# Two hybrid decoder layers on one core: linear attention's buffers laid on those of the attention's projections, its gates split by token half, and an earlier, wider spaced stream of cache pages

## The chip, the cores and the metric

The kernel runs on one core of one Trainium2 chip. The metric is the device time of one execution in microseconds; lower is better. Runs of the kernel before agree within 0.1%.

## What is computed

Two consecutive layers of a decoder, for a prompt of 1024 tokens and for 8 single sample tokens that share the weights, all in float32 (each large product is made of three matmuls on split high and low halves). The core of the reference, for the prompt:

```python
n = rmsnorm(yp, norm1[l])
q, k, v, gq, gk, gv, glog, gg = project(n, w_in[l], ...)      # one input projection, two groups of heads
od = diff_attn_prompt(q, k, v, lam)        # softmax(q1 k1^T) - lam * softmax(q2 k2^T), times v; 4 heads
og, s_fin = gla_prompt(gq, gk, gv, glog)   # S_t = diag(alpha_t) S_{t-1} + k_t^T v_t;  o_t = q_t S_t; 4 heads
yp = yp + merge(od, og, gg, ...)           # og -> rmsnorm(og) * silu(gg); concat(od, og) @ w_out
yp = yp + ffn(yp, norm2[l], w_gu[l], w_down[l])               # (silu(a) * b) @ w_down, width 2816
```

The 8 sample tokens go through the same layer; their attention reads 1024 past keys and values each from a paged cache (8 pages of 128 rows x 512 per token, for keys and for values), and their linear attention updates a given state by one step.

## The kernel before

Tiles are handed out by pools with a compile-time scheduler: instructions are issued on each engine in the order in which a simulated run finds them ready, the lowest priority number first. A pool with `reuse_waits="tile"` lets a new tile wait only for the old tiles that lay on the same bytes or banks. Pools are stacked from the left of the on-chip memory, and from the right with `side="right"`, so the order in which they are opened decides what lies on what.

Each layer (`layer`, L265) has three stages.

- **Attention** (`phase_d`, L383): for each of 4 heads, 9 projection tiles (`psq`, weights in `wDr`, `wDh`, `wDl`: raw, high half, low half), and two tiles later scores (`psS`), softmax, transposes (`tpw`) and the product with v (`po`). Its banks are `psS` 0 to 2, `psT` 3 and 4, `psg` 5 to 7.
- **Linear attention** (`phase_g`, L605): products for q and k (`psqk`), v (`psv`) and the gate (`psgg`), all from pool `psgg`, with weights in `wGr`, `wGh`, `wGl`; log gates, six levels of decay masks (`gla_a`), the chunk recurrence (`gla_o`), a norm per token half (`gate_norm`, `psgn`), and the product with silu of the gate. For the second pair of heads the gate of all tokens is kept in `gqs[0]`, and `gate_mul(t)` applies it to the token half t. The order of these calls is written out at the end of the function. `PIECES` cuts the tokens into 512, 260 and 260 (the 8 sample tokens are the last).
- **Out-projection and feed-forward**, for tokens 0 to 511 and then for the other 520 (`out_half`, `ffn_half`). Here priorities are planned times: `dense(us)` (L100) gives each weight tile its place on a clock of TensorE time (2.8 us for half an out-projection tile, 5.6 for a tile of the gate or up product, 0.7 per row block of the down product), and `mix(us)` (L104) the place of the sample tokens' work on the same clock. `prep_tile` loads a weight tile over SP into `raw` (3 buffers), casts its high half on ACT into `wh` and its low half on DVE into `wl`, and notes the three instructions in `marks`; `behind(slot)` queues an instruction behind the one noted for the current place, on the same engine.

`decode` (L1090) runs beside the first half's feed-forward, from `MIX_START` on the planner's clock: 64 key pages (load over SP, product with `qbd` on GpSimd, reduction `sall` on DVE), the softmax over all, 64 value pages (even ones on ACT and GpSimd, odd ones on DVE, summed in `vacc`), and twice `sample_gla`, the state step of two heads (loads of the states `S0` and of `vb`, four products and sums on GpSimd, a store). Its pool `dec` lies at the right, below the accumulators of the out-projection. The 8 tokens' result `osf` goes into the second half's `out_half`, whose pool `op` lies on the bytes of `dec`.

Of the kernel before, what the change touches and what calls it, by code (L numbers as in the profile page):

```python
# [10 lines left out]
F32 = mybir.dt.float32  # L11
# [7 lines left out]
PSUM = bass.MemoryType.PSUM  # L19
DRAM = bass.MemoryType.DRAM  # L20

P = 128
# [9 lines left out]
WM = HALF + NB  # L32
PIECES = ((0, HALF), (HALF, HALF + WM // 2), (HALF + WM // 2, TOK))
TICK = 20
MIX_START = 58.0
DEPTH = 2
PAST = 1024
NPG = 8
# [2 lines left out]
DK = 64  # L41
DV = 128
RANK = 16
NPB = 6
LAG = 2
GRH = 3
VPOOL = (0, 2, 4, 6)
# [15 lines left out]
def hybrid_kernel(  # L63
# [201 lines left out]
    def layer(l):  # L265
        sn = smp.tile([NB, 2 * H], F32, name="sn", tag="sn")
        osf = smp.tile([P, 2 * H, NB], F32, name="osf", tag="osf")
        smc = smp.tile([P, 2, 3, NB], F32, name="smc", tag="smc")
        gsm = smp.tile([P, H, NB], F32, name="gsm", tag="gsm")
        if l:  # L270
            sample_cols()

        with ExitStack() as octx:
            with ExitStack() as mix_:
                pgp = mix_.enter_context(tc.tile_pool(name="pgp", bufs=1, reuse_waits="tile", side="right"))
                with ExitStack() as dctx:
                    wa2 = phase_d(l, dctx, sn, pgp)
                ogb = octx.enter_context(tc.tile_pool(name="ogb", bufs=1, reuse_waits="tile"))
                og1 = ogb.tile([P, H, WM], F32, name="og1", tag="og1")
                oga = octx.enter_context(ExitStack())  # L280
                ogp = oga.enter_context(tc.tile_pool(name="oga", bufs=1, reuse_waits="tile"))
                og0 = ogp.tile([P, H, HALF], F32, name="og0", tag="og0")
                ogs = (og0, og1)
                with ExitStack() as gctx:
                    phase_g(l, gctx, ogs, smc, gsm, wa2)
            with ExitStack() as pctx:
                psD = pctx.enter_context(tc.tile_pool(name="psD", bufs=2, space=PSUM, reuse_waits="tile"))
                psn = pctx.enter_context(tc.tile_pool(name="psn", bufs=2, space=PSUM, reuse_waits="tile"))
                psX = pctx.enter_context(tc.tile_pool(name="psX", bufs=2, space=PSUM, reuse_waits="tile"))
                wps = [pctx.enter_context(tc.tile_pool(name=n, bufs=1, reuse_waits="tile", side="right")) for n in ("wFr", "wFh", "wFl")]  # L290
                span_start()
                with ExitStack() as fctx:
                    with ExitStack() as actx:
                        ac = new_acc(actx)
                        acc = out_half(l, 0, og0, osf, ac, wps, psD)
                        oga.close()
                        ffn_half(l, 0, acc, ac, wps, psD, psn, fctx)
                        clock["mix"] = MIX_START
                        decode(l, actx, osf, smc, gsm, psX)
                    actx = pctx.enter_context(ExitStack())  # L300
                    ac = new_acc(actx)
                    acc = out_half(l, 1, og1, osf, ac, wps, psD)
                ffn_half(l, 1, acc, ac, wps, psD, psn, actx)
                span_end()
# [298 lines left out]
        return wa2  # L603

    def phase_g(l, gctx, ogs, smc, gsm, wa2):  # L605
        psg = gctx.enter_context(tc.tile_pool(name="psgg", bufs=2, space=PSUM, reuse_waits="tile"))
        gp, gpd, gl, ge_, wr, wh_, wl_, gqp, gb_ = [gctx.enter_context(tc.tile_pool(name=n, bufs=1, reuse_waits="tile"))
                                          for n in ("gp", "gpD", "gpL", "gpE", "wGr", "wGh", "wGl", "gqp", "gpB")]
        wp = (wr, wh_, wl_)
        psA = gctx.enter_context(tc.tile_pool(name="psA", bufs=2, space=PSUM, reuse_waits="tile"))  # L610
        psO = gctx.enter_context(tc.tile_pool(name="psOg", bufs=1, space=PSUM, reuse_waits="tile"))
        psX = gctx.enter_context(tc.tile_pool(name="psXg", bufs=1, space=PSUM, reuse_waits="tile"))
        psT = gctx.enter_context(tc.tile_pool(name="psTg", bufs=2, space=PSUM, reuse_waits="tile"))

        gr = ssq[0:RANK, :]
        gqs = [(pl.tile([P, TOK], F32, name=f"gq{p}", tag=f"gq{p}"), pl.tile([P, TOK], F32, name=f"gk{p}", tag=f"gk{p}"))
# [211 lines left out]

        gws = {}

        def gate_proj(p, e):
            store = p == 1
            if p not in gws:
                gws[p] = prep_cols(wp, l, C_GG + p * 256, 1, 256, 256, q=w_queues[2])
            Hs, Ls = gws[p]
            for t, (ca, cb) in enumerate(PIECES):
                n = cb - ca
                ps = psg.tile([P, 512], F32, name="psgg", tag="g")
                gemm_feat(ps, e * P, Hs, Ls, t)
                y = gqs[0][e][:, ca:cb] if store else gpd.tile([P, HALF], F32, name="gy", tag="gy", bufs=1)[:, :n]  # L840
                tt(y, ps[:, :n], rstd[:, ca:cb], ALU.mult)
                a = gb_.tile([P, 512], F32, name="gya", tag="gsq", bufs=2)[:, :n]
                act(a, y, AF.Abs)
                act(a, a, AF.Exp, scale=-1.0)
                act(a, a, AF.Ln, bias=1.0)
                stt(a, y, 0.0, a, ALU.min, ALU.subtract)
                act(a, a, AF.Exp)
                tt(y, y, a, ALU.mult)
                if t == 2:
                    DVE.tensor_copy(gsm[:, 2 * p + e, :], y[:, n - NB:n])  # L850
                if not store:
                    m = n - (NB if t == 2 else 0)
                    o = ogs[0][:, 2 * p + e, :] if t == 0 else ogs[1][:, 2 * p + e, ca - HALF:ca - HALF + m]
                    tt(o, o, y[:, :m], ALU.mult)
# [27 lines left out]
        gla_o(1, 1, 0)  # L882
        gla_o(1, 1, 1)
        gate_norm(1, 0)
        gate_proj(1, 0)
        gate_proj(1, 1)
        gate_mul(0)
        gate_norm(1, 1)
        gate_mul(1)

    def new_acc(st):
# [195 lines left out]

    def decode(l, st, osf, smc, gsm, psX):  # L1090
        cp = st.enter_context(tc.tile_pool(name="dec", bufs=1, reuse_waits="tile", side="right"))
        sall = cp.tile([P, NPG, NB, 2 * H], F32, name="sall", tag="sall")
        wall = cp.tile([P, NPG, 32], F32, name="wall", tag="wall")
        wnb = cp.tile([P, 32], F32, name="wnb", tag="wnb")
# [6 lines left out]

        def decode_k(b):
            qb = cp.tile([P, 512], F32, name="qbd", tag="qb", bufs=2)
            SP.dma_start(qb, scr_q[l][b:b + 1, :].to_broadcast([P, 512]))
            for j in range(NPG):
                mix(2.1)
                pg = page(cache_k[l], b, j)
                tt(pg, pg, qb, ALU.mult, POOL)
                with behind(3, 1):
                    DVE.tensor_reduce(out=sall[:, j, b, :], in_=pg.rearrange("p (h d) -> p h d", d=DK), axis=AX.X, op=ALU.add)  # L1110
# [4 lines left out]
        def sample_gla(p):  # L1115
            q, k, eg = (smc[:, p, a, :] for a in range(3))
            sh = [P, 4, DV]
            vbs = []
            for b0 in (0, 4):
                bs = slice(b0, b0 + 4)  # L1120
                S0 = cp.tile(sh, F32, name="S0", tag="S0", bufs=1)
                vb = cp.tile(sh, F32, name="vb", tag="vb", bufs=2)
                for e in range(2):
                    h = 2 * p + e
                    SP.dma_start(S0[64 * e:64 * e + 64], state_gla[l, bs, h].rearrange("b d v -> d b v"))
                    SP.dma_start(vb[64 * e:64 * e + 64],
                                 scr_gv[l][bs, h * DV:(h + 1) * DV].unsqueeze(0).to_broadcast([64, 4, DV]))
                tt(S0, S0, bc(eg[:, bs].unsqueeze(2), sh), ALU.mult, POOL)
                tt(vb, vb, bc(k[:, bs].unsqueeze(2), sh), ALU.mult, POOL)
                tt(S0, S0, vb, ALU.add, POOL)  # L1130
                for e in range(2):
                    SP.dma_start(gla_sample[l, bs, 2 * p + e].rearrange("b d v -> d b v"), S0[64 * e:64 * e + 64])
                tt(vb, S0, bc(q[:, bs].unsqueeze(2), sh), ALU.mult, POOL)
                vbs.append(vb)

            def out():
                ps = psx("pss")
                pv = ps[:, 0:16].rearrange("p (b e) -> p b e", e=2)
                for b in range(NB):
                    mm(pv[:, b, :], vbs[b // 4][:, b % 4, :], hsel, True, True)  # L1140
                DVE.tensor_copy(osf[:, H + 2 * p:H + 2 * p + 2, :], pv.rearrange("p b e -> p e b"))

            return out
# [41 lines left out]
            tt(osd, pn[:, 32:64].rearrange("p (h b) -> p h b", h=H), wnb.rearrange("p (b h) -> p h b", h=H), ALU.mult)  # L1185

        def decode_v(b):
            acc = cp.tile([P, H, DV], F32, name="vacc", tag="prod", bufs=4)
            accp = cp.tile([P, H, DV], F32, name="vaccp", tag="qb", bufs=2)
            first = {0: True, 1: True}  # L1190
            for j in range(NPG):
                mix(2.1)
                pg = page(cache_v[l], b, j)
                w4 = wall[:, j, b * H:(b + 1) * H]
                p4 = pg.rearrange("p (h d) -> p h d", h=H)
# [42 lines left out]
        for b in range(NB):  # L1238
# [1 line left out]
            if len(ready) > 2:  # L1240
                ready.pop(0)()
            if b in (1, 4):
                mix(6)
                gla = sample_gla(b // 4)
            if b in (3, 6):
                gla()
# [79 lines left out]
```

## Time and profile before

| | us |
|---|---|
| runs (median, lowest, highest of 3) | 2836.69, 2835.61, 2837.54 |
| the profiled execution, its own time | 2846.13 |
| its span, first to last instruction | 2844.3 |
| TensorE matmul busy | 2723.1 (96%) |
| VectorE (DVE) busy | 1804.5 (63%) |
| ScalarE (ACT) busy | 1361.1 (48%) |
| GpSimd (POOL) busy | 386.3 (14%) |
| mean granted TensorE clock | 0.985 |

Layer 0 runs to about 1425 us and layer 1 from there on. In layer 0 the attention ends near 312, the linear attention near 539, the first token half near 996. TensorE is the engine that the others serve; a stretch in which its busy time falls short of the stretch, or in which its granted clock is below 1, is where time is lost. A line of the timeline gives start, duration, engine, source line, operation, output and inputs, the count of equal instructions that follow one another, and in brackets how long the engine had been idle and what ended that.

### The profile page before, as it was taken

How to read it: one execution, taken by the hardware profiler on the slowest of the kernel's cores; microseconds unless marked ns; L12 is line 12 of the kernel's file. 1: busy time of each engine (PE TensorE's matmuls, PEld its weight loads, DVE VectorE, ACT ScalarE, POOL GpSimd, SP SyncE). 2: the span in 40 equal slices, each digit the busy share in tenths (PEclk: the TensorE clock that was granted, in tenths of full speed). 3: DMA queues.
4: the chain of work that ended last, by engine and by line, in shares of the span. 5: the costliest groups of instructions: out<-in, count | busy, mean ns of one | idle time of the engine just before them, and what ended most of it. 6: DMA issues, size and time to landing. Idle time of an engine off the chain costs nothing.

```text
span 2844.3 us, 46804 instructions
## 1 busy us (share of the span) xinstructions
PE 2723.1 (96%) x16906; PEld 2406.7 (85%) x16906; DVE 1804.5 (63%) x3549; ACT 1361.1 (48%) x3343; POOL 386.3 (14%) x333
## 2 busy tenths in 40 slices
PE   7999899998999999999999999999999999999999
PEld 6887788777788799999988878877677888999999
DVE  6777676568877564444478765775678765544444
ACT  7888445532455343222278883464324453322222
POOL 1000000046433000000020000000663320000000
PEclk9999999999999999999999999999999999999999
DMA  4121111266666342333222111112666664333332
GB/s 132 55 62 36 52 32 44 68 176 210 208 190 195 103 133 83 96 91 96 71 53 58 41 36 47 31 47 84 201 208 205 178 189 137 93 91 90 96 90 83
DMA packets 461322, 298.13 MB, mean 105 GB/s; under 512 B 34698, under 2 KB 416906, under 8 KB 461090
## 3 DMA queue, kind: packets, MB, share of 16 engines
q1 hardware_dynamic: 452322, 290.90, 34.6%
q10 hardware_dynamic: 8704, 4.20, 0.5%
q8 instruction: 134, 2.20, 0.3%
q14 instruction: 98, 0.80, 0.1%
q0 software_dynamic: 64, 0.03, 0.0%
HBM read 271.53 MB, written 23.53 MB: 104 GB/s over the span
## 4 chain that ended last, share of the span: by engine, by line
PE 72%; DVE 12%; ACT 8%; issue 3%; DMA 3%; POOL 2%; SPq 0%; DVEq 0%; ACTq 0%; POOLq 0%
PE psd L82 51%; PE psq L82 4%; PE psv L82 3%; PE psqk L82 3%; DVE wl L135 2%; PE psgg L82 2%; PE po L82 2%; ACT sc L88 2%; POOL page L135 1%; ACT qn L88 1%; ACT qhh L88 1%; PE poG L82 1%; PE psS L82 1%; PE tpw L85 1%; DMA page<-in_cache_k 1%
## 5 line engine op out<-in xcount | busy, mean ns | idle before, releaser
L88 ACT ACTIVATE wh<-raw 128x512 fp32r<-128x512 f32 (+1 forms) x608 | 354.1, 615 | 937.8 <-PE psd L82 697.2
L82 PE MATMUL psd<-xH,wl 128*128 128x260 f32 (+1 forms) x2112 | 681.0, 322 | 16.0 <-DVE wl L135 16.0
L82 PE MATMUL psd<-xH,wh 128*128 128x260 f32 (+1 forms) x2112 | 677.9, 321 | 0.0
L82 PE MATMUL psd<-xL,wh 128*128 128x260 f32 (+1 forms) x2112 | 676.8, 321 | 1.0 <-DVE xL L138 1.0
L135 DVE TENSOR_TENSOR wl<-raw,wh 128x512 fp32r<-128x512 f32 (+1 forms) x608 | 454.2, 764 | 90.3 <-issue 51.4
L82 PEld LDWEIGHTS psd<-xH,wl 128*128 128x128 f32 x2112 | 398.5, 189 | 53.2 <-DVE wl L135 22.0
L82 PEld LDWEIGHTS psd<-xL,wh 128*128 128x128 f32 x2112 | 398.1, 188 | 34.2 <-DVE xL L138 2.7
L82 PEld LDWEIGHTS psd<-xH,wh 128*128 128x128 f32 x2112 | 398.0, 189 | 30.2 <-issue 0.5
L82 PE MATMUL psd<-hh,wl 128*128 128x260 f32 (+1 forms) x1056 | 341.6, 323 | 15.4 <-DVE wl L135 15.1
L82 PE MATMUL psd<-hh,wh 128*128 128x260 f32 (+1 forms) x1056 | 340.5, 322 | 1.0 <-DVE acc L135 1.0
L82 PE MATMUL psd<-hl,wh 128*128 128x260 f32 (+1 forms) x1056 | 339.7, 322 | 0.0
L82 PEld LDWEIGHTS psd<-hh,wl 128*128 128x128 f32 x1056 | 200.5, 190 | 35.5 <-DVE wl L135 21.2
L135 DVE TENSOR_TENSOR acc<-psd,acc 128x520 f32<-128x520 f32 (+1 forms) x144 | 125.7, 873 | 163.0 <-PE psd L82 162.8
L82 PEld LDWEIGHTS psd<-hh,wh 128*128 128x128 f32 x1056 | 200.5, 190 | 15.4 <-issue 1.3
L82 PEld LDWEIGHTS psd<-hl,wh 128*128 128x128 f32 x1056 | 200.4, 190 | 14.3
L135 POOL TENSOR_TENSOR page<-page,qbd 128x512 f32<-128x512 f32 x128 | 191.5, 1521 | 59.4 <-DMA page<-in_cache_k 41.9
L82 PE MATMUL psq<-wh,xH 128*128 128x384 f32 (+1 forms) x512 | 178.7, 349 | 6.6 <-DVE zs L135 3.1
L82 PE MATMUL psq<-wh,xL 128*128 128x384 f32 (+1 forms) x512 | 178.3, 349 | 0.0
L82 PE MATMUL psq<-wl,xH 128*128 128x384 f32 (+1 forms) x512 | 177.6, 347 | 0.0
L135 DVE TENSOR_TENSOR sa<-psd,rstd 128x520 f32<-128x520 f32 (+1 forms) x66 | 57.6, 873 | 180.2 <-PE psd L82 176.1
L135 DVE TENSOR_TENSOR tb<-psd,rstd 128x520 f32<-128x520 f32 (+1 forms) x66 | 57.6, 873 | 152.2 <-PE psd L82 152.2
L138 DVE SCALAR_TENSOR_TENSOR wl<-raw,g1c,wh 128x256 fp32r<-128x256 f32 (+2 forms) x160 | 80.7, 537 | 88.4 <-ACT wh L88 52.6
(330 smaller groups left out, 5386.1 us busy)
## 6 DMA issues: line engine op xcount, KB each, us to landing
raw<-in_w_gu SPq DMA_DIRECT2D x176, 512.0 KB
raw<-in_w_down SPq DMA_DIRECT2D x160, 256.0 KB
page<-in_cache_k SPq DMA_DIRECT2D x128, 256.0 KB
page<-in_cache_v SPq DMA_DIRECT2D x128, 256.0 KB
raw<-in_w_out SPq DMA_DIRECT2D x32, 512.0 KB
raw<-in_w_in SPq DMA_DIRECT2D x64, 192.0 KB
raw<-in_w_in SPq DMA_DIRECT2D x64, 128.0 KB
xt<-in_x_prompt SPq DMA_DIRECT2D x8, 512.0 KB
```

What stands on the lines that cost most here:

```text
L82: PE.matmul(out, lhsT=lhsT, rhs=rhs, start=start, stop=stop, skip_group_check=True)
L85: PE.matmul(out, lhsT=in_, rhs=ident[:n, :n], is_transpose=True)
L88: return ACT.activation(out, in_, func, **kw)
L135: return (eng or DVE).tensor_tensor(out, a, b, op=op)
L138: (eng or DVE).scalar_tensor_tensor(out=out, in0=in0, scalar=scalar, in1=in1, op0=op0, op1=op1)
```

## The change

Four things are changed.

1. In `phase_g` the pools of the masks and decay buffers (`gl`, `ge`) are opened after the weights, `gqp` and `gpB` instead of before, so that weights and `gqp` move down by their 14 KB. The psum pool `psgg` is opened last instead of first: its two banks become 6 and 7 instead of 0 and 1, and the four others move down by two.
2. `gate_proj` takes the pieces that it is to make. For the second pair of heads the piece of the first token half is made for both columns, then the norm of the second half, `gate_mul(0)`, and then the other pieces.
3. `decode` gets its pool from the caller, which opens it before the first out-projection; the value accumulators are three tiles of their own instead of four of a ring, and page buffers are 5 instead of 6, so that the pool is 4 KB smaller.
4. The sample work starts at 24 instead of 58 on the planner's clock, with 2.6 us instead of 2.1 for each page. The loads of `qbd`, `S0` and `vb` are queued behind the weight load of their place; the state's place is 5 us for each half of the tokens instead of 6 ahead of both; the state's store is queued behind the weight load due 10 us later.

```diff
-MIX_START = 58.0
+MIX_START = 24.0
-NPB = 6
+NPB = 5
@@ layer
                         ac = new_acc(actx)
+                        cp = actx.enter_context(tc.tile_pool(name="dec", bufs=1, reuse_waits="tile", side="right"))
                         acc = out_half(l, 0, og0, osf, ac, wps, psD)
...
-                        decode(l, actx, osf, smc, gsm, psX)
+                        decode(l, cp, osf, smc, gsm, psX)
@@ phase_g
-        psg = gctx.enter_context(tc.tile_pool(name="psgg", bufs=2, space=PSUM, reuse_waits="tile"))
-        gp, gpd, gl, ge_, wr, wh_, wl_, gqp, gb_ = [gctx.enter_context(tc.tile_pool(name=n, bufs=1, reuse_waits="tile"))
-                                          for n in ("gp", "gpD", "gpL", "gpE", "wGr", "wGh", "wGl", "gqp", "gpB")]
+        gp, gpd, wr, wh_, wl_, gqp, gb_, gl, ge_ = [gctx.enter_context(tc.tile_pool(name=n, bufs=1, reuse_waits="tile"))
+                                          for n in ("gp", "gpD", "wGr", "wGh", "wGl", "gqp", "gpB", "gpL", "gpE")]
...
         psT = gctx.enter_context(tc.tile_pool(name="psTg", bufs=2, space=PSUM, reuse_waits="tile"))
+        psg = gctx.enter_context(tc.tile_pool(name="psgg", bufs=2, space=PSUM, reuse_waits="tile"))
...
-        def gate_proj(p, e):
+        def gate_proj(p, e, ts=(0, 1, 2)):
...
-            for t, (ca, cb) in enumerate(PIECES):
+            for t in ts:
+                ca, cb = PIECES[t]
...
         gate_norm(1, 0)
-        gate_proj(1, 0)
-        gate_proj(1, 1)
+        gate_proj(1, 0, (0,))
+        gate_proj(1, 1, (0,))
+        gate_norm(1, 1)
         gate_mul(0)
-        gate_norm(1, 1)
+        gate_proj(1, 0, (1, 2))
+        gate_proj(1, 1, (1, 2))
         gate_mul(1)
@@ decode
-        cp = st.enter_context(tc.tile_pool(name="dec", bufs=1, reuse_waits="tile", side="right"))
+        vaccs = [cp.tile([P, H, DV], F32, name=f"vacc{z}", tag=f"vacc{z}") for z in range(3)]
@@ decode_k
-            SP.dma_start(qb, scr_q[l][b:b + 1, :].to_broadcast([P, 512]))
+            with behind(1):
+                SP.dma_start(qb, scr_q[l][b:b + 1, :].to_broadcast([P, 512]))
             for j in range(NPG):
-                mix(2.1)
+                mix(2.6)
@@ sample_gla, for each half of the tokens
+                mix(5)
+                with behind(1):
+                    for e in range(2):
+                        h = 2 * p + e
+                        SP.dma_start(S0[64 * e:64 * e + 64], state_gla[l, bs, h].rearrange("b d v -> d b v"))
...
-                for e in range(2):
-                    SP.dma_start(gla_sample[l, bs, 2 * p + e].rearrange("b d v -> d b v"), S0[64 * e:64 * e + 64])
+                with tc.issue_after(mark_at(clock["mix"] + 10)[1].ins):
+                    for e in range(2):
+                        SP.dma_start(gla_sample[l, bs, 2 * p + e].rearrange("b d v -> d b v"), S0[64 * e:64 * e + 64])
@@ decode_v
-            acc = cp.tile([P, H, DV], F32, name="vacc", tag="prod", bufs=4)
+            acc = vaccs[b % 3]
...
-                mix(2.1)
+                mix(2.6)
@@ the loop over value requests
             if b in (1, 4):
-                mix(6)
                 gla = sample_gla(b // 4)
```

## Rows read from the trace of the kernel before

**Rows 1.** The page's engine line: busy us, share of the span, instructions.
```profile
PE 2723.1 (96%) x16906; PEld 2406.7 (85%) x16906; DVE 1804.5 (63%) x3549; ACT 1361.1 (48%) x3343; POOL 386.3 (14%) x333
```

**Rows 2.** Busy by stretch: PE, PEld, DVE, ACT, POOL (count); PEclk, DMA share, GB/s.
```profile
284.00:355.00 71.00, 60.20 (x354) 50.87 (x354) 46.50 (x105) 33.67 (x70) 5.80 (x10) 0.93 0.18 52
```

**Rows 3.** TensorE's waits, 287 to 319: us in total, times, longest.
```profile
PE tpw L85 <- DVE sc L138: 3.7, 2, 3.2
PE psqk L82 <- DVE wl L138: 3.2, 1, 3.2
PE psN L82 <- ACT sqo L88: 1.1, 1, 1.1
```

**Rows 4.** Timeline of TensorE: behind the wait, and 4 us later.
```profile
315.49 0.63 PE L82 MATMUL psqk<-xH,wl 128*128 128x512 f32 x1
315.92 0.63 PE L82 MATMUL psqk<-xH,wh 128*128 128x512 f32 x1
...
319.08 0.39 PE L82 MATMUL psqk<-xL,wh 128*128 128x512 f32 x1
319.31 0.40 PE L82 MATMUL psqk<-xH,wl 128*128 128x512 f32 x1
```

**Rows 5.** TensorE's waits at the same place of layer 1, 1694 to 1726.
```profile
PE psqk L82 <- DVE wl L138: 4.3, 1, 4.3
```

**Rows 6.** Timeline of DVE and of ACT at the end of attention.
```profile
313.13 1.67 DVE L138 SCALAR_TENSOR_TENSOR wl<-raw,g1c,wh 128x256 fp32r<-128x256 f32 x4
...
306.46 0.39 ACT L88 ACTIVATE oraw<-po 128x256 f32<-128x256 f32 x1 [4.62 <-PE po L82]
```

**Rows 7.** Busy by stretch, and timeline of TensorE, into the first out-projection.
```profile
530.00:547.00 17.00, 10.97 (x25) 6.29 (x24) 8.26 (x16) 9.39 (x18) 0.00 (x0) 0.70 0.23 63
1937.00:1954.00 17.00, 11.46 (x27) 6.65 (x26) 8.38 (x16) 9.51 (x19) 0.00 (x0) 0.60 0.22 62
...
532.98 3.61 PE L82 MATMUL psgn<-gsq,ones_dv 128*128 128x512 f32 x4 [2.60 <-ACT gsq L88]
539.06 0.50 PE L82 MATMUL psd<-oHb,wh 128*128 128x512 f32 x1 [2.48 <-ACT wh L88]
```

**Rows 8.** Timeline of SP and of ACT: the out-projection's weights.
```profile
456.68 0.43 SPq L896 DMA_DIRECT2D raw<-in_w_out  x1
...
537.88 3.22 ACT L88 ACTIVATE wh<-raw 128x512 fp32r<-128x512 f32 x6
```

**Rows 9.** TensorE's waits, 568 to 710, then 1975 to 2150 (layer 1).
```profile
PE psd L82 <- DVE wl L135: 13.1, 7, 5.0
...
PE psd L82 <- DVE wl L135: 14.3, 10, 4.6
```

**Rows 10.** Timeline of GpSimd, DVE and TensorE while key pages stream.
```profile
609.61 1.04 POOL L135 TENSOR_TENSOR vb<-vb,smc 128x512 f32<-128x512 f32 x1 [2.70 <-DMA vb<-scr_gv]
...
615.44 0.69 DVE L1110 TENSOR_REDUCE sall<-page 128x8 f32<-128x512 f32 x1 [6.04 <-POOL page L135]
...
676.59 1.04 POOL L135 TENSOR_TENSOR S<-S,smc 128x512 f32<-128x512 f32 x1 [4.96 <-DMA S<-in_state_gla]
...
683.15 0.63 PE L82 MATMUL psd<-hh,wl 128*128 128x512 f32 x1 [4.10 <-DVE wl L135]
```

**Rows 11.** DVE's casts, 545 to 569 (GpSimd idle) and 595 to 760.
```profile
L135 DVE TENSOR_TENSOR wl<-raw,wh 128x512 fp32r<-128x512 f32 x7 | 4.6, 686 | 12.7 <-issue 9.9 <-PE psd L82 2.8
...
L135 DVE TENSOR_TENSOR wl<-raw,wh 128x512 fp32r<-128x512 f32 x51 | 55.4, 1106 | 9.6 <-issue 5.3 <-DMA vb<-scr_gv 2.4 <-ACT wh L88 1.8
```

**Rows 12.** Timelines of SP, ACT, TensorE at decode's end; SP's waits, 585 to 760.
```profile
902.71 0.33 SPq L312 DMA_DIRECT2D page<-in_cache_v  x1
...
936.61 0.21 ACT L88 ACTIVATE oHa<-osf 128x32 fp32r<-128x32 f32 x1
...
998.78 0.59 PE L82 MATMUL psd<-oHb,wh 128*128 128x260 f32 x1 [2.20 <-ACT wh L88]
...
SPq L312 <- DVE sall L1110: 15.7, 13, 3.2
```

More of the change, by code (lines that the diff above doesn't have):

```diff
@@ L1086, in ffn_half, with decode @@
         down(end, he)
-    def decode(l, st, osf, smc, gsm, psX):
-        cp = st.enter_context(tc.tile_pool(name="dec", bufs=1, reuse_waits="tile", side="right"))
+    def decode(l, cp, osf, smc, gsm, psX):
+        vaccs = [cp.tile([P, H, DV], F32, name=f"vacc{z}", tag=f"vacc{z}") for z in range(3)]
         sall = cp.tile([P, NPG, NB, 2 * H], F32, name="sall", tag="sall")
@@ L1122, in sample_gla @@
                 vb = cp.tile(sh, F32, name="vb", tag="vb", bufs=2)
-                for e in range(2):
[L1124 to L1127, printed above, removed]
+                mix(5)
[3 more added lines that the diff above has]
+                        SP.dma_start(S0[64 * e:64 * e + 64], state_gla[l, bs, h].rearrange("b d v -> d b v"))
+                        SP.dma_start(vb[64 * e:64 * e + 64],
+                                     scr_gv[l][bs, h * DV:(h + 1) * DV].unsqueeze(0).to_broadcast([64, 4, DV]))
                 tt(S0, S0, bc(eg[:, bs].unsqueeze(2), sh), ALU.mult, POOL)
@@ L1130, in sample_gla @@
                 tt(S0, S0, vb, ALU.add, POOL)
-                for e in range(2):
-                    SP.dma_start(gla_sample[l, bs, 2 * p + e].rearrange("b d v -> d b v"), S0[64 * e:64 * e + 64])
+                with tc.issue_after(mark_at(clock["mix"] + 10)[1].ins):
+                    for e in range(2):
+                        SP.dma_start(gla_sample[l, bs, 2 * p + e].rearrange("b d v -> d b v"), S0[64 * e:64 * e + 64])
                 tt(vb, S0, bc(q[:, bs].unsqueeze(2), sh), ALU.mult, POOL)
```

## The prediction, made before the change was run

> **What bounds the kernel now.** I read the page's engine line first, then the busy time by stretch, then TensorE's waits in the stretches where it falls short, then the timeline inside those. TensorE is busy 96% of the span, every other engine 63% or less [rows 1]. So what can be won is TensorE's idle time and the slow clock after it. Both stand in three places of each layer: where attention hands over to the linear attention (71 - 60.2 = 10.8 us idle in 284 to 355, granted clock 0.93) [rows 2], where the linear attention hands over to the out-projection, and in the first third of the first half's feed-forward, while key pages stream. The change touches these three and takes no work off TensorE, so the sum is three terms per layer. [...]
>
> **Term 1: attention to linear attention.** TensorE waits 3.7 us for the last score rows, 1.1 for their norm, and 3.2 for `wl`, the low half of the first q/k weights [rows 3]: 8.0 us. Behind the last gap some eight 512-column matmuls lose 0.2 us each, and narrow ones and the last `po` run at half pace; with 3.5 us for this (an estimate from [rows 4]) the place costs 11.5 us in layer 0. Layer 1 waits 4.3 for the same casts [rows 5]; I count 11 there.
> Why does the work behind it not fill this? The first `wl` casts run at 313.13, four in one block [rows 6]. Before, most of `wGl` and all of `gqp` lie on attention's buffers (pool `dpB`) and `psgg` on the score banks (`psS`), in use until the last head is finished. After, the weight pools, `gqp` and the gemm banks lie inside those of attention's own projection (`wDr`, `wDh`, `wDl`, `psg`), whose last matmul comes before attention's last two tiles. So eight casts on ACT and eight on DVE, at some 0.45 us each, can be done in gaps such as ACT's 4.62 us wait for `po` [rows 6], and 22 us of `psqk` matmuls (48 of 512 columns at 0.23 us and 96 of 260 at half that) are there as filler. But `raw` has four buffers for eight weight rows, its loads are issued by ACT in order, and ACT carries attention's tail; the early gaps fill in part. I take three quarters: 9 us and 8 us. Bounds: the whole 11.5 and 11; on the other side a loss of 4, when casts stand ahead of attention's tail (8 x 0.45 on either chain) and nothing is covered. The masks and decay buffers (`gl`, `ge`, `gpB`) now lie on attention's buffers instead; their first use stands behind the q/k product, so I cost that at nothing under this cover, and at 3 us without it.
>
> **Term 2: linear attention to out-projection.** In 17 us here TensorE idles 6.0 at a granted clock of 0.70, in layer 1 5.5 at 0.60; the two long waits are 2.60 for the late norm and 2.48 for the first out-projection weight cast [rows 7]. About 12 matmuls then run 0.2 us slow each, and the norm's four 1.5 us in all: 6.0 + 2.3 + 1.5 = 9.8 us, and 9.7 in layer 1. The weights are not late: the third load was issued at 456.7, and the cast waits until 537.9 [rows 8], since `wFl` and one slot of `wFh` lie on `gpB`. After, they lie on `gl` and `ge`, which are done before the last gates. The gate product is split: first token half of both columns, then the second norm and `gate_mul(0)`, then the other pieces. Those are 96 matmuls of 260 columns at half the 0.23 us of [rows 4], 11 us of cover for a gate chain of some 7 us, the late norm and the casts to `oHb`. The out-projection's banks become `psA`, `psO` and `psX`, free by then. All of it can go; I take 8 per layer for what the written order still leaves, bounds 4 and 9.8. Nothing is removed: the same matmuls and casts are issued.
>
> **Term 3: the page stream.** TensorE waits 13.1 us for `wl` in layer 0 and 14.3 in layer 1 [rows 9]. The chain: GpSimd serves `sample_gla`, whose loads nothing held back, ahead of the first key pages (609.61); DVE, in order, idles 6.04 us for the first page product (615.44), and the weight cast queued behind that misses TensorE by 5.0 us [rows 9, 10]. The same at 676.59: GpSimd waits 4.96 for a late state load, and TensorE 4.10 at 683 [rows 10]. The change puts the state loads behind their due weight load in the value phase and paces pages at 2.6 us instead of 2.1, from 24 instead of 58 on the planner's clock. The key phase thus ends as before (58 + 64 x 2.1 = 192; 24 + 64 x 2.6 = 190). The two stalls with their slow clock (1.7 each) are 5.0 + 4.1 + 3.4 = 12.5 us; of the smaller ones I count 2 as gone.
> Against that, pages now run beside the out-projection. Its DVE work per pair of output tiles, 11.2 us of TensorE, is four casts at 0.69 [rows 11] and some 5.3 us of adds and sums (two of twice the cast's width, four of the same): 8.1 us. With GpSimd busy a cast takes 1.11 [rows 11]; if the other operations with two SBUF inputs stretch alike it is 11.5 us, and 4.3 page reductions at 0.69 [rows 10] make 14.4, over by 3.2 us for some pair and a half: 4 us lost, after what the weight buffers hide. One more is for state loads in the value phase (one buffer; a load waits for the delayed store). Net 12.5 + 2 - 5 = 9.5; I take 8. Bounds: 17, when all waits go and the out-projection keeps its pace, and -3, when stalls only move there.
> [...]
> Edits that I cost at nothing: five page buffers instead of six (5 x 2.6 = 13.0 us of hold, 6 x 2.1 = 12.6), three accumulators instead of four (each is read two requests later, 21 us apart each), `qb` and the stores behind weight loads. Cover: weight loads run two to three tiles ahead; without it, each blocks SP and the weights queued behind it, priced in the third rival.
>
> **Sum.** 9 + 8 + 2 x 8 + 2 x 8 = 49 us. The profiled execution took 2846.13 us (span 2844.3 and 1.8 around it), so it would become 2797. The median of the runs is 9.4 lower, 2836.69; the same 49 off it is 2788.
>
> **Rivals.**
> First, **the early q/k product stays late**: the casts remain queued behind attention's last operations, because ACT is full there. For it: DVE cast all four rows it had only after attention's end, in one block [rows 6]. Against: the memory reason for that is gone. Without term 1: 2837 - 32 = 2805. Chance 0.15.
> Second, **DVE becomes the bound in the out-projection**: every pair of output tiles from the first page on waits for DVE, 3.2 us over per pair, and the feed-forward's up products, whose DVE work stretches too, fall behind; term 3 goes to zero: 2837 - 33 = 2804. For it: [rows 11]; against: the gate products that follow leave DVE time to catch up. Chance 0.17.
> Third, the other sign: **decode ends too late**. The second half's `op` pool lies on `dec`'s tiles, so its loads of `oHa` wait for the last pages and accumulators. Before, the last page was issued at 902.7, the sample outputs were cast at 936.6, and TensorE took the second out-projection at 998.8 [rows 12]. The last page moves from 344.8 to 382.8 on the planner's clock, so the cast goes to about 975, 24 us of slack. Past that each microsecond is one on TensorE. To lose all 49 us both layers must slip by 24 + 24.5 = 48 us, 0.38 us on each of 128 pages, a hold of 14.9 us per page buffer instead of 13.0. SP already waited 15.7 us for page buffers in the key phase [rows 12], though with stalls that now go. At 15.0 us of hold per page: 2842. Chance 0.05.
> Fourth, **all cover works**: 11.5 + 11 + 19.5 + 34 = 76, 2761. Chance 0.10.
> My forecast, 2788 and 10 either way: 0.53.
>
> **How the numbers follow.** The range takes the forecast, the first two rivals and the near part of the fourth: 2764 to 2816; both first rivals at once give 2821 and stand outside it. A measurement of this kernel tells apart 0.2%, 5.7 us. Slower by more: 0.04, the third rival past its point. Within: 0.04, its edge and the first two rivals with a slip of decode on top. Faster: 0.92.
>
> **What would show it.** Right: `psqk` matmuls among the last `po` and `tpw`, the first `wl` cast before 295, no `psqk` wait of 3 us; after the last `psgg` the first `psd` within 1 us, and w_out casts well before it; no `sample_gla` on GpSimd before the value phase, and waits of `psd` for `wl` below 6 us per layer there. Wrong: `psd` waiting for `wl` during the out-projection by more than 8 us, or a gap ahead of the second half's first `psd` that ends on `oHa` or `osf`.

## The result, and the profile after

The changed kernel takes 2794.86 us (median of 4 runs, 2793.89 to 2798.4), the kernel before 2837.11 in runs beside it: a ratio of the two times of 0.985, 95% interval 0.9833 to 0.9867, or 42.6 us (38 to 47). Forecast were 2788 and 49 us.

The profiled execution took 2795.14 us with a span of 2793.3, against 2846.13 and 2844.3. That pair differs by 51 us: the profiled execution of before was a long one, as the first experiment shows. The table cuts the spans at TensorE's own matmuls: the first and the last `psq`, the first `psgg`, and the first and the last `psd` on `oHb` of each token half. The column in the middle is that first experiment, the kernel before once more. Here and below, two numbers with a stroke are layer 0 and layer 1.

| stage, us (layer 0 / layer 1) | before | before, again | after |
|---|---|---|---|
| attention's projections to their end | 268.6 / 264.5 | 269.3 / 264.2 | 270.8 / 264.5 |
| from there to the first `psgg` | 173.3 / 175.2 | 172.7 / 173.8 | 164.1 / 165.8 |
| first `psgg` to the out-projection | 85.7 / 84.5 | 84.5 / 84.3 | 79.1 / 78.9 |
| first half's out-projection | 44.8 / 44.3 | 43.4 / 43.6 | 42.8 / 41.4 |
| first half's feed-forward, with decode | 414.9 / 414.9 | 416.0 / 409.2 | 407.9 / 402.4 |
| second half's out-projection | 46.5 / 44.7 | 46.8 / 44.7 | 48.4 / 44.6 |
| the rest of the layer | 376.8 / 389.9 | 377.4 / 389.5 | 377.4 / 389.9 |

First come the engine line and the two handovers by stretch; the columns are those of [rows 1, 2, 7]. The last two stretches end 6 to 7 us behind the first `psd`, those of [rows 7] nearly 8.

```profile
PE 2709.5 (97%) x16906; PEld 2403.9 (86%) x16906; DVE 1824.9 (65%) x3549; ACT 1358.8 (49%) x3343; POOL 403.0 (14%) x333
...
284.00:355.00 71.00, 66.15 (x431) 57.36 (x432) 48.34 (x113) 36.99 (x78) 7.19 (x13) 1.00 0.19 55
515.00:532.00 17.00, 16.97 (x110) 15.01 (x109) 10.33 (x23) 10.45 (x23) 1.76 (x1) 1.00 0.10 32
1900.00:1917.00 17.00, 16.98 (x110) 14.90 (x109) 11.58 (x23) 11.12 (x24) 1.30 (x1) 1.00 0.10 32
```

Same matmuls, 13.6 us less busy time: they ran at the higher clock. The granted clock is 1.00 where it was 0.93, 0.70 and 0.60, and the two 17 us stretches hold no idle time where 6.0 and 5.5 us stood.

At the first handover, TensorE, ACT and DVE by start time, then TensorE's waits there in layer 0 (287 to 312) and layer 1 (1660 to 1680):

```profile
286.54 0.39 PE L82 MATMUL psqk<-xH,wh 128*128 128x512 f32 x1
286.77 0.33 PE L82 MATMUL psS<-kt,qhh 128*128 128x384 f32 x1
...
285.21 0.90 ACT L88 ACTIVATE wh<-raw,g1c 128x256 fp32r<-128x256 f32 x2
290.08 0.87 DVE L138 SCALAR_TENSOR_TENSOR wl<-raw,g1c,wh 128x256 fp32r<-128x256 f32 x2
...
PE psqk L82 <- ACT wh L88: 1.7, 1, 1.7
PE psqk L82 <- DVE wl L138: 2.3, 1, 2.3
```

The first `wl` cast runs at 290.08 instead of 313.13 [rows 6], and q/k products stand between the last scores. At the second handover, the last gate matmul and the first of the out-projection:

```profile
525.10 0.28 PE L82 MATMUL psgg<-xH,wl 128*128 128x260 f32 x1
525.22 0.39 PE L82 MATMUL psd<-oHb,wh 128*128 128x512 f32 x1
```

There is no gap, against 2.48 us before [rows 7]. The out-projection's weights are cast some 60 us ahead of it, on ACT, where the first such cast ran at 537.88 before [rows 8]:

```profile
466.05 1.13 ACT L88 ACTIVATE wh<-raw 128x512 fp32r<-128x512 f32 x2
```

Behind the handover, TensorE's waits from 568 to 697 in layer 0, then from 1952 to 2080 in layer 1:

```profile
PE psd L82 <- DVE xL L138: 2.2, 2, 1.5
PE psd L82 <- ACT xH L88: 1.8, 1, 1.8
PE psd L82 <- DVE wl L135: 1.3, 2, 0.9
...
PE psd L82 <- DVE xL L138: 2.0, 2, 1.4
PE psd L82 <- ACT xH L88: 1.7, 1, 1.7
PE psd L82 <- DVE wl L135: 0.5, 1, 0.5
```

These two windows begin where the first out-projection ends. In the stretches that match those of [rows 9], which begin some 29 us behind its first `psd`, the waits for `wl` are 2.5 and 1.3 us instead of 13.1 and 14.3. New ones for `xL` and `xH`, the out-projection's own results, stand at the first gate products of the feed-forward. GpSimd now takes the state's first product in the value phase, at 767.03; before, it took it at 605.87, ahead of all key pages:

```profile
767.03 1.04 POOL L135 TENSOR_TENSOR S<-S,smc 128x512 f32<-128x512 f32 x1 [2.37 <-DMA S<-in_state_gla]
```

### The profile page after: what moved, and what is told of

The parts are those of the page before. It is cut to its first block, busy times and chain, and to the rows that moved or that the text cites. A ratio compares the mean times of both kernels' runs of the same rounds, so it can differ in the third digit from the quotient of the medians.

```text
span 2793.3 us, 46822 instructions
## 1 busy us (share of the span) xinstructions
PE 2709.5 (97%) x16906; PEld 2403.9 (86%) x16906; DVE 1824.9 (65%) x3549; ACT 1358.8 (49%) x3343; POOL 403.0 (14%) x333
## 4 chain that ended last, share of the span: by engine, by line
PE 78%; DVE 10%; ACT 8%; issue 2%; DMA 2%; SPq 0%; POOL 0%; ACTq 0%; DVEq 0%; POOLq 0%
PE psd L82 56%; PE psq L82 4%; PE psqk L82 3%; PE psv L82 3%; PE psgg L82 2%; PE po L82 2%; ACT sc L88 2%; PE psA L82 1%; DVE wl L135 1%; PE psS L82 1%; ACT qn L88 1%; PE poG L82 1%; ACT qhh L88 1%; PE tpw L85 1%; DVE acc L135 1%
## 5 line engine op out<-in xcount | busy, mean ns | idle before, releaser
L135 DVE TENSOR_TENSOR wl<-raw,wh 128x512 fp32r<-128x512 f32 (+1 forms) x608 | 443.9, 746 | 72.8 <-issue 41.3
L82 PEld LDWEIGHTS psd<-hh,wh 128*128 128x128 f32 x1056 | 199.2, 189 | 14.6 <-issue 1.3
L82 PEld LDWEIGHTS psd<-hl,wh 128*128 128x128 f32 x1056 | 198.8, 188 | 13.6
```

Of the source, the lines that this page charges most:

```text
L82: PE.matmul(out, lhsT=lhsT, rhs=rhs, start=start, stop=stop, skip_group_check=True)
L135: return (eng or DVE).tensor_tensor(out, a, b, op=op)
```

## The experiments

Each run has a ratio of its time to that of the kernel before in runs beside it; savings are worked out from the ratio and its interval, taken of 2837 us, and two runs are compared by their ratios. The kernel before varies more than the three runs at the start showed: 19 of its runs lie between 2833.7 and 2845.1 us, 0.4%. "Loss" in a stretch is the sum, over TensorE's matmuls, of the time from one start to the next above the lower quartile of that shape in the same trace; so it holds idle time and slow clock.

**Which part gives what.** The kernel before again, and each part alone.

> The kernel before, once more, for a second profile. Its profiled execution took 2846.1 us, 9 above the median of its runs, and the changed kernel's profile is 51.0 shorter while the medians differ by 42.2. Theory: the first profile of the kernel before holds about 9 us that its usual execution has not, and the stage where it stands is the layer 1 feed-forward while pages stream (459.2 us for the first half there, 15.4 longer than after, against 9.0 in layer 0); then this profile ends near 2837 and that stage takes about 450 to 453. Rival: profiles of this kernel are always some 9 us long; then 2846 again and 459 again.

Its profile took 2836.2 us, 10 less than the first, and 5.7 of that stand in layer 1's feed-forward (409.2 against 414.9). So the stage table's first column flatters the page stream; the runs decide on it.

```diff
 p1_pools: before, with
-        psg = gctx.enter_context(tc.tile_pool(name="psgg", bufs=2, space=PSUM, reuse_waits="tile"))
...
-                                          for n in ("gp", "gpD", "gpL", "gpE", "wGr", "wGh", "wGl", "gqp", "gpB")]
...
+                                          for n in ("gp", "gpD", "wGr", "wGh", "wGl", "gqp", "gpB", "gpL", "gpE")]
...
+        psg = gctx.enter_context(tc.tile_pool(name="psgg", bufs=2, space=PSUM, reuse_waits="tile"))
```

> Only the pools of the linear attention (weights below the masks, psgg opened last). Theory, three separate places that add: both layers' way from attention to the linear attention shortens by 9.2 and 9.4 as in the full change, and of the way to the out-projection the share of the late weight cast, 2.5 of idling and as much of slow clock per layer is gone too: 18.6 + 7 = 26 saved, 2811. Rival 1 (early product is not what the pools give, order set elsewhere): below 5 saved, 2832 or more. Rival 2 (the idle time in front of the out-projection only changes its name, since the norm is late as well): 18.6 saved, 2818.

2802.53 us, ratio 0.9868 (0.9851 to 0.9885): 37 us saved (33 to 42), 11 more than expected. Attention's projections to the first `psgg`: 162.6 / 163.9. From there to the out-projection: 76.7 / 75.7. All of the idle time at the second handover went, not only the cast's half:

```profile
522.51 0.39 PE L82 MATMUL psd<-oLb,wh 128*128 128x512 f32 x1
522.96 1.12 PE L82 MATMUL psgn<-gsq,ones_dv 128*128 128x512 f32 x2
523.52 0.79 PE L82 MATMUL psd<-oHb,wl 128*128 128x512 f32 x1
```

The late norm's matmuls (`psgn`) run among those of the out-projection. That norm belongs to the second token half, which the first out-projection does not read; once the weights are cast, there is work for TensorE while the norm's chain runs on ACT.

```diff
 p2_split: before, with
-        gate_proj(1, 0)
-        gate_proj(1, 1)
-        gate_mul(0)
-        gate_norm(1, 1)
+        gate_proj(1, 0, (0,))
+        gate_proj(1, 1, (0,))
+        gate_norm(1, 1)
+        gate_mul(0)
+        gate_proj(1, 0, (1, 2))
+        gate_proj(1, 1, (1, 2))
```

> Only the gates by token half. Theory: the late norm's idling goes (2.6 us, and 1.5 of slow matmuls, per layer), while the out-projection's weights still wait for the buffers of the gate product; 6 saved in all, 2831. Rival 1: without the buffers the split gains nothing, because the cast that waits for the last use of those buffers ends the stretch in any order: 0, 2837. Rival 2: the split alone does the whole of that place, 12 saved, 2825.

2836.17 us, ratio 0.9984 (0.9973 to 0.9994): 4.5 us (2 to 8), near the theory. The wait for the norm is gone and the one for the cast is longer, 4.4 us where it was 2.48 [rows 7]:

```profile
PE psd L82 <- ACT wh L88: 4.4, 1, 4.4
```

p3_stream has parts 3 and 4 of the change, and before's pools and gate order:

```diff
+MIX_START = 24.0
...
+NPB = 5
...
+                        cp = actx.enter_context(tc.tile_pool(name="dec", bufs=1, reuse_waits="tile", side="right"))
...
+                mix(2.6)
...
+                mix(5)
+                with behind(1):
...
```

> Only the sample work: decode's pool early, start at 24, 2.6 us a page, state loads behind their weight loads. Theory: with the pools and the split taken out, term 3 remains, 42.2 - 26 - 6 = 10 saved, 2827, if the surplus of the first profile of the kernel before belongs to that stage. Rival 1: the surplus is real and this part gives 22, 2815. Rival 2: the parts need each other (pages from the out-projection on are hidden only behind a full queue): 5 or less, 2832.

2831.6 us, ratio 0.9973 (0.9961 to 0.9984): 7.7 us (4.5 to 11). The parts alone add to 49, all together give 42.6. The pools and the stream without the split add to 45, and the run without the split (below) gives 44.8: the split's part is a wait that the pools take away as well, so it counts but once.

**Memory or banks.** Each of the two edits of p1_pools by itself: the middle pair of lines of its diff (the order in on-chip memory), and the outer pair (`psgg` opened last).

> The kernel before with the order of the pools in on-chip memory alone; the psum pool psgg stays first. Theory: memory for the weights gates both places. The out-projection's first cast no longer waits, so the way from the first gate product to it takes 77 us as with both edits (84 to 86 before); the q/k weights are cast early, but the products still wait for the score banks, so from attention's last projection to the first gate product it takes some 168 us (173 to 175 before, 163 to 164 with both). 26 saved, about 2812. Rival: the banks are what gates the early product and the out-projection's start: 5 or less saved, 2833.

2811.07 us, ratio 0.9912 (0.9895 to 0.993): 25 us. It takes 168.8 / 168.6 us to the first `psgg` and 76.5 / 77.5 from there to the out-projection, as the theory had it. The out-projection's first weights are cast at 468.39. In 284 to 355 the idle time is between those of before and of both edits, and no wait for `wl` is left; the waits there are for the scores and the norm (`sc` 4.6 us, `sqo` 1.9):

```profile
284.00:355.00 71.00, 63.79 (x393) 54.93 (x393) 46.06 (x105) 34.16 (x70) 7.03 (x13) 0.93 0.18 52
```

> The kernel before with psgg opened last, and nothing else. Theory: without memory for the weights the banks bring nothing: both ways as before (173 to 175 and 84 to 86 us), 0 to 3 saved, 2836. Rival: the banks alone bring the early product, 163 to 164 us and 84 to 86, 20 saved, 2818.

2839.06 us, ratio 1.0001 (0.9991 to 1.0011): nothing. `psqk` waits 5.0 us for `wl`, and the out-projection's first cast runs at 540.15, as late as before (with the split alone it is 536.31). So the order in memory alone moves that cast. Free banks are worth half of the first handover, and only behind early casts.

**Is the split needed?** The changed kernel with the lines of p2 undone.

> The changed kernel with the gates by token half undone: pools and page stream alone. In the profile of the pools alone the way from the first gate product to the out-projection takes 76.7 and 75.7 us, in the full change 79.1 and 78.9. Theory: the split gives nothing on top of the pools and gives back those 2.4 and 3.2, since it puts the second half's norm ahead of the out-projection where nobody waits for it: 5 to 6 saved against the changed kernel, 2789. Rival: the split is needed once the pages run beside the out-projection (DVE then is late with the last gates): 2 to 4 lost, 2798.

2790.93 us, ratio 0.9842 (0.9826 to 0.9857). Its interval overlaps the changed kernel's: neither the gain of the theory nor the loss of the rival is shown. In its trace the norm's matmuls lie in the out-projection again, which takes 45.1 / 44.0 instead of 42.8 / 41.4, and the way there is 2.4 / 3.1 shorter. What the split moves out of one stage it puts into the other.

**What stalled the page stream.** All on the changed kernel. r_hold has the old start and pace:

```diff
-MIX_START = 24.0
+MIX_START = 58.0
...
-                mix(2.6)
+                mix(2.1)
```

> The changed kernel with the old start and pace of the pages (58 and 2.1 us), state loads still held back to the value phase. Theory 1 (the stalls of the key phase came from the state's work on GpSimd): they stay away, and the out-projection has no pages beside it: 2795, within 4 of the changed kernel, TensorE's loss 80 to 130 us behind the out-projection below 3 us per layer (8 before, 1 to 2 after). Theory 2 (they came from the pace): they come back, 6 or more there per layer, 2805 or more.

2794.12 us, ratio 0.984 (0.9827 to 0.9854), the same as the changed kernel. The loss 80 to 130 us behind the out-projection is 1.6 / 2.2. So what this part gives comes with what r_hold keeps of it, the held loads above all (r_free, below); start and pace together add nothing. They do act, but their effects cancel: without them TensorE loses less in the out-projection and at the first gate products (table below), and a new stall appears in the value phase, 177 to 250 us behind the out-projection (8.3 in both layers, 1.4 and 1.4 in the changed kernel; the profiled run is 7 us above this kernel's median). SP's waits from 755 to 800 name it:

```profile
SPq L1140 <- POOL S L135: 10.9, 2, 8.2
```

The state's store waits 8.2 us for GpSimd's sum, and weight loads stand behind it on SP.

r_free has the early start and wide pace, and the state's loads and stores unheld, as before:

```diff
-                mix(5)
-                with behind(1):
...
-                with tc.issue_after(mark_at(clock["mix"] + 10)[1].ins):
...
```

> The changed kernel with the state's loads and stores free again as before, pages still from 24 at 2.6 us. Theory 1 (the state's work stalled the stream): GpSimd takes the state's products early, each waits for its load and holds the pages behind it, 4 to 8 us lost per layer: 2803 to 2811. Theory 2 (pace): no stall comes back, 2795 within 3.

2813.08 us, ratio 0.9903 (0.9886 to 0.9921): by the ratios 15 us above the changed kernel, as theory 1 has it, but at another place than it thought: the out-projection is 56.8 / 55.9 us long. GpSimd, then DVE, by start time:

```profile
532.97 1.22 POOL L135 TENSOR_TENSOR S<-S,smc 128x512 f32<-128x512 f32 x1 [68.39 <-DMA S<-in_state_gla]
...
547.73 8.46 POOL L135 TENSOR_TENSOR page<-page,qbd 128x512 f32<-128x512 f32 x5 [7.73 <-DMA qbd<-scr_q]
...
553.30 3.43 DVE L135 TENSOR_TENSOR wl<-raw,wh 128x512 fp32r<-128x512 f32 x2
```

GpSimd takes the state's products first, then the held-up page products in bunches: `qbd`, which they need, is loaded on SP behind the state's loads and stores, at 543.56 instead of 525.90 in the changed kernel. Beside a bunch two casts take 3.43 us, 1.37 alone (2 x 0.686). Which weighs more, GpSimd's order or that of SP's loads, this run doesn't tell.

r_noprod leaves out GpSimd's product of each key page with the query; loads, reductions and everything else stay.

```diff
-                tt(pg, pg, qb, ALU.mult, POOL)
```

> The changed kernel without GpSimd's product of the key pages with the query (that part of the computation is left out; loads and reductions stay). In the changed kernel the out-projection's sums and splits on DVE take 1.50 and 1.47 us, 0.69 and 0.75 without GpSimd. [...]

2778.14 us, ratio 0.9782 (0.9767 to 0.9797): by the ratios 19 us below the changed kernel. Expected were 8 to 10 us, 2786, from sums and splits back at 0.7 us, and less than 3, 2792 or more, should the reductions or the chain of sums be what TensorE waits for. DVE's operations from 545 to 569, first in the changed kernel, then in this one (form, count, busy us, mean ns):

```profile
L135 DVE TENSOR_TENSOR wl<-raw,wh 128x512 fp32r<-128x512 f32 x8 | 6.7, 861 | 0.2 <-PE psd L82 0.2
L135 DVE TENSOR_TENSOR ssq<-ssq,nsq 128x512 f32<-128x512 f32 x4 | 6.0, 1503 | 0.0
L1115 DVE TENSOR_REDUCE sall<-page 128x8 f32<-128x512 f32 x8 | 5.1, 671 | 0.0
L138 DVE SCALAR_TENSOR_TENSOR xL<-acc,g2c,xH 128x512 fp32r<-128x512 f32 x3 | 4.2, 1405 | 0.0
...
L1114 DVE TENSOR_REDUCE sall<-page 128x8 f32<-128x512 f32 x11 | 7.0, 676 | 0.0
L135 DVE TENSOR_TENSOR wl<-raw,wh 128x512 fp32r<-128x512 f32 x10 | 6.6, 686 | 5.6 <-PE psd L82 3.3 <-DMA page<-in_cache_k 2.2
L138 DVE SCALAR_TENSOR_TENSOR xL<-acc,g2c,xH 128x512 fp32r<-128x512 f32 x4 | 3.0, 742 | 0.0
L135 DVE TENSOR_TENSOR ssq<-ssq,nsq 128x512 f32<-128x512 f32 x4 | 2.7, 684 | 0.0
```

With GpSimd's products DVE has 0.2 us of idle time in these 24 us; without them the sums (`ssq`) and splits (`xL`) take half as long, and DVE does more reductions and casts with time to spare. TensorE's loss by kernel follows; 14.6 of the 19 us are in the middle column.

| | in the out-projection | next 57 us | next 73 us |
|---|---|---|---|
| before | 6.2 / 5.8 | 10.5 / 10.2 | 10.1 / 9.2 |
| p1_pools | 3.9 / 3.9 | 9.9 / 9.9 | 10.0 / 9.3 |
| p3_stream | 9.5 / 6.9 | 7.5 / 9.2 | 1.1 / 1.5 |
| after | 4.4 / 2.9 | 10.5 / 9.7 | 2.4 / 1.3 |
| r_hold | 2.2 / 2.2 | 8.3 / 3.7 | 2.0 / 2.5 |
| r_noprod | 2.6 / 2.5 | 2.8 / 2.8 | 0.8 / 0.8 |
| b1 (below) | 3.9 / 3.9 | 3.2 / 3.4 | 5.5 / 4.6 |

**A faster version.** b1 is p1_pools with the state's loads held, the pages at their old start, and room for the store.

```diff
 b1: p1_pools, with
-NPB = 6
+NPB = 5
...
+            with behind(1):
+                SP.dma_start(qb, scr_q[l][b:b + 1, :].to_broadcast([P, 512]))
...
-                mix(2.1)
+                mix(2.4)
...
-                S0 = cp.tile(sh, F32, name="S0", tag="S0", bufs=1)
+                S0 = cp.tile(sh, F32, name="S0", tag="S0", bufs=2)
...
+                mix(5)
+                with behind(1):
...
+                with tc.issue_after(mark_at(clock["mix"] + 20)[1].ins):
...
```

> A version meant to beat both: the pools alone (no split), the pages at their old start 58 with 2.4 us instead of 2.1, five page buffers, state loads held back to the value phase as in the change, its store 20 us behind instead of 10 and two state buffers instead of one, and decode's pool opened where it was before. Theory: the out-projection runs without GpSimd beside it (40.7 us instead of 42.8 and 41.4 in the changed kernel), no stall in the key phase, and none for the state's store, which held SP for 8 us in the run with the old start and pace (8.3 us of TensorE's loss there per layer): 10 below that run's 2794, and 3 more without the split: 2782. Rival: pages that start later only move GpSimd's products beside the next stage and decode ends later: 2791 or more.

2775.62 us (5 runs, 2770.2 to 2781.72), ratio 0.9779 (0.9764 to 0.9794): 63 us saved, 20 more than the change, and the intervals are apart. The out-projection has no GpSimd beside it, and the stretch behind it loses 3.2 / 3.4 instead of 10.5 / 9.7. Two things came otherwise than expected: the out-projection takes 43 us and not 40.7, since without the split the late norm's matmuls lie in it, and the key phase loses 5.5 / 4.6 us, more than in r_hold. TensorE's waits in those 57 us of layer 0:

```profile
PE psd L82 <- DVE wl L135: 0.5, 1, 0.5
PE psd L82 <- DVE xL L138: 0.5, 2, 0.3
```

b2 puts the sums of squares at the end of layer 0's halves on DVE.

```diff
-                        new_x(acc, ac, X, j, eng=POOL)
+                        new_x(acc, ac, X, j)
```

> The faster version before (pools, pages from 58 at 2.4 us, held state loads), with the sums of squares at layer 0's two ends on DVE instead of GpSimd. At the first half's end TensorE loses 7 us in the last 40 us ahead of the second out-projection, in every kernel so far, while DVE's splits into xL take 1.4 to 1.8 us beside GpSimd's sums and 0.69 alone. [...]

2785.86 us, ratio 0.9805 (0.9792 to 0.9818): 7 slower than b1 (the intervals just touch). Expected was 2773, 2 to 4 us gained, or 2779, as much lost, should the sums lengthen DVE's chain; the result is on the side of the loss. DVE from 945 to 975, b1, then b2:

```profile
L135 DVE TENSOR_TENSOR xL<-acc,xH 128x512 fp32r<-128x512 f32 x8 | 8.8, 1111 | 0.4 <-ACT xH L88 0.3
...
L135 DVE TENSOR_TENSOR xL<-acc,xH 128x512 fp32r<-128x512 f32 x8 | 5.4, 688 | 0.5 <-ACT xH L88 0.4
L135 DVE TENSOR_TENSOR ssq<-ssq,nsq 128x512 f32<-128x512 f32 x7 | 4.8, 688 | 1.1 <-ACT nsq L88 1.1
```

The splits are back at 0.69 us, 3.4 us in all, but the sums cost 4.8 on the engine that is the chain there. The second out-projection grows from 45.1 to 49.4 us.

## Why the prediction was right, and where not

The sign, the range and the three places were right; 42.6 us came where 49 were forecast. By its steps:

- **Term 1** (17 us): 9.2 and 9.4 in the stage table, 18.6 (16.6 against the second profile of before). The chain is the forecast's: casts in attention's gaps, then products as filler. Its three quarters hold; ACT and DVE in attention's tail are what is left (1.7 and 2.3 us of waits). q1 and q2 show both edits at work, memory first.
- **Term 2** (16 us): 6.6 and 5.6 to the first `psd` in the stage table, and 2.0 and 2.9 more in the out-projection itself, 17.1 in all; against the second profile of before it is 5.4 and 5.4, and 0.6 and 2.2, 13.6 in all. The waits went wholly, near the size forecast. The step that failed is what to credit: the forecast let the split cover the late norm and the casts. The pools alone do all of it, since a weight that is cast in time lets the out-projection cover the norm. Beside the pools the split's effect is below what the runs tell apart.
- **Term 3** (16 us): the mis-sized one. The part alone gave 7.7 us (4.5 to 11). In the changed kernel's trace the first half's feed-forward is 8.1 and 6.8 us shorter than in the second profile of before, and layer 0's second out-projection 1.6 longer, 13 us in all; so the term lies somewhere between 8 and 13. The stall of 4.10 us at 683 and what lies around it went, as forecast (loss 10.1 / 9.2 to 2.4 / 1.3). The 1.7 us of slow clock counted for each stall fit the trace of before: behind the one at 683, matmuls start eight times 0.43 us apart and once 0.34 until they are back at 0.23, which makes 1.7 us at a granted clock of 0.57 (683 to 687), and behind the one of 5.0 us it is 2.0 us at 0.52 (624 to 629); in the changed kernel the clock is 1.00 from 600 to 700. The step that failed is the price of 5 us per layer, 4 of it in the out-projection: the forecast had DVE over by 3.2 us per pair there and let the gate products give DVE its time back. The out-projection hardly paid. It loses about what it does with the pools alone (4.4 / 2.9 against 3.9 / 3.9), with 2.8 / 1.4 us of waits for `wl` against the 8 that would have been wrong, and in the part alone it lost 3.3 and 1.1 us more than before, within the 4 allowed for. The first gate products, which need `xL` at once, paid instead. The 5.0 us there [rows 9, 10] was counted as gained, but the loss of that stretch stayed, 10.5 / 10.2 to 10.5 / 9.7: the wait for `wl` became one for `xL` and `xH`. Without GpSimd's products it is 2.8 / 2.8, and the run is 19 us faster (r_noprod), which puts the price at up to 9.5 us per layer. The gain was counted too low too, 14.5 us per layer (12.5 + 2) where the loss behind the out-projection falls by 17.0 / 15.8 without the products. That these two misses cancel in part is luck.
- **Rival 2** was so half right, with its place one stage late. The removed product shows it (r_noprod, 19 us). The forecast's price of 1.11 us per operation was taken from the casts: these took 0.86, but sums and splits 1.50 and 1.41.
- **Rival 3** did not come. The last value page was issued 8.5 us later than before and the cast for the second half 16.3 us later, 23.0 us ahead of the second out-projection, which by then starts 22.9 us earlier itself (62.2 ahead before, [rows 12]; the forecast had 24). So against the out-projection the cast slipped by 39 us, and the forecast had 38:

```profile
911.25 0.33 SPq L313 DMA_DIRECT2D page<-in_cache_v  x1
...
952.93 0.21 ACT L88 ACTIVATE oHa<-osf 128x32 fp32r<-128x32 f32 x1
...
975.93 0.59 PE L82 MATMUL psd<-oHb,wh 128*128 128x260 f32 x1 [1.32 <-ACT wh L88]
```

- Of the edits costed at nothing, the held store costs nothing only with the new start and pace: with the old ones (r_hold) it blocked SP for 8.2 us. Five page buffers and three accumulators were not tried by themselves, so no run shows their price.

Left open: what the stream's part is worth more closely than 8 to 13 us, and how much of b1's gain over r_hold is the missing split, the pace or the second state buffer; these were not taken apart.

## What to carry to other kernels

Ask first on whose memory the next stage's weights lie: opening pools in another order gave 37 us by itself, where the whole change gave 43, without an instruction added or removed, and no gain of the hand-written reordering beside it can be told apart. A wait ahead of a handover hides others; price them together, since whatever ends last can be covered by the work that the first release sets free. When a helper engine's work is moved earlier to thin it out, look at which operations of its neighbour stretch beside it (here DVE's sums, from 0.68 to 1.50 us) and which later stage needs their results at once: there the bill comes.

## What the runs showed of the hardware

DVE's sums and splits, which have two inputs in on-chip memory, took about twice as long beside GpSimd's products in the out-projection (sums 0.684 to 1.503 us, splits 0.742 to 1.405 on average), while reductions (0.676 and 0.671) and sums with an input in psum (`acc<-psd,xH`, 1.21 both) did not change. The longest single sums took 1.78 us, near the 1.72 of one sum and one GpSimd product, one after the other (0.68 and 1.04 [rows 10]); why they take that long was not shown. It takes an overlap, too: the wide sums `acc<-acc,xL`, with both inputs in on-chip memory, kept 1.21 us in the changed kernel, where no product ran beside them, and took up to 2.28 us in r_free, where some did. What had not been expected is what this comes to on TensorE: leaving out the products of the key pages gave 19 us of 2795, with GpSimd busy 14% of the span.
